# Order of the next stage's weight casts, a short chain moved to GpSimd, and a one-row product made square, in a two-layer hybrid decoder step

## The chip, the core and the metric

The kernel runs on one core of a Trainium2 chip. The metric is the device time of one execution in microseconds (us). Three runs of the kernel before gave 1076.46, 1076.46 and 1078.43 us, so the median is 1076.46 us.

## The reference, cut to what matters

A trunk of two layers is applied to 256 prompt tokens and 8 single sample tokens, so 264 columns in all, with 1024 features. Each layer is

```python
h = layer_norm(DN_ALPHA * x + 0.5 * swiglu(x, f1g, f1u, f1d), ln1_g, ln1_b)
mix = mixer(h, ...)                 # gated DeltaNet on 4 heads beside causal pooling
h = layer_norm(DN_ALPHA * h + mix, ln2_g, ln2_b)
y = layer_norm(DN_ALPHA * h + 0.5 * swiglu(h, f2g, f2u, f2d), ln3_g, ln3_b)

def swiglu(x, wg, wu, wd):
    return (jax.nn.silu(x @ wg) * (x @ wu)) @ wd
```

The hidden width of the SwiGLU is 2816. In the mixer every token and head has a decay

```python
g = -jnp.exp(a_log) * jax.nn.softplus(a_raw + dt_bias)
```

whose running sum inside a chunk sets the factors of the scores, and the mixer ends in `concatenate([o_dn, o_pool]) @ w_out`. All inputs are float32.

## The kernel before, in words

Features lie on the 128 partitions and tokens on the free axis, so an activation is eight tiles of 128 x 264. Every product is done in three parts in the type fp32r: each operand is split into a rounded high part and a low remainder (`mm3`, lines 220 to 223: high times high, high weight times low input, low weight times high input).

**Weights.** `Weights.load` brings a unit of 1 MB from memory into one of three `wraw` buffers by a transfer on the queue of SyncE, and splits its two pieces: the high part by a copy on ScalarE (`whi` or `xhi`, line 180), the low part by a subtraction on VectorE (`wlo` or `xlo`, line 185). `W.ahead(n)` loads until n pieces are ready and not yet taken by `W.get`. Pieces named `x..` are the first five of a stage and have buffers of their own; the others share three pairs. `W.after` and `W.after_hi` name an instruction of VectorE and of ScalarE behind which the subtractions and copies of the loads that follow are queued on that engine.

**Order of work.** TensorE runs its instructions in the order in which the source gives them. The other engines' orders are made by a planner from priorities (place in the source, raised inside `tc.high_priority()`) and from its own costs, and each engine then runs its queue in that fixed order.

**End of a feed-forward block** (`ffn`). Eight output tiles `pd` are made in turn, each of 22 x 3 matmuls with 22 pieces of the down weights in all. After each tile the residual sum is made in `X` (line 299, VectorE), and `Norm.shifted` makes from it `RH` (line 272, ScalarE), `RL` (line 273, VectorE), the square `sq` (lines 269 and 276, ScalarE), and the sums over tiles `acc1` (line 283) and `acc2` (line 285). `RH` and `RL` are the high and low parts of the sum before normalisation. The next stage starts on them at once: `raw_products` multiplies the first weight pieces by tiles that are already there, and `stats` (lines 345 and 346) then turns `acc1` and `acc2` into mean and variance by two products with ones. In a mixer the order is: 21 matmuls of the first piece `x0`, the statistics, then pieces `x1` to `x3`. In the feed-forward block of layer 1 it is: 24 matmuls that take turns between `x0` and `x1`, the statistics, then the rest.

At the tile m = 6 the kernel before calls `W.ahead(6)`. There 1 piece is ready, so three units are loaded: the last two of the down weights and the first of the next stage (`x0`, `x1`). After the last tile `W.ahead(4)` loads the second (`x2`, `x3`).

**The decay.** In the mixer, after the products of `q` tile 0 and pooling tile 3, the softplus is worked out on 128 x 12 numbers (lines 649 to 673): exponentials on ScalarE, and on VectorE a quotient `s_` (lines 662 to 664), a polynomial `p_` of its square `y_` (lines 665 to 669) and the sum `xa` (671) and product `gg` (673). From `gg` come `gp` (677, 678), the masked tiles `gm` (709) and four-head products `pdiff` (719) on TensorE. In the source these lie between four `q` and four pooling products; the convolutions `c` (line 528) and low parts `wlo` (185) run on VectorE meanwhile, and the window sums `wsum` (line 617) on GpSimd. `dm` (628 to 633) on VectorE reads `wsum`.

**The shift.** Eight output products `pop` (`w_pool`) of a layer start with `norm.less_shift`, a product that adds one row `less` (1 x 264) to all partitions: its stationary operand is one row of ones of `gto`. It has one row of contraction.

Of the kernel before, what the change touches and what calls it, by code (L numbers as in the profile page):

```python
# [10 lines left out]
F32R = mybir.dt.float32r  # L11
AF = mybir.ActivationFunctionType
ALU = mybir.AluOpType
# [3 lines left out]
P = 128  # L17
D = 1024
KD = D // P
SEQ = 256  # L20
NB = 8
T = SEQ + NB
# [3 lines left out]
H = 4  # L26
ALPHA = (2.0 * DEPTH) ** 0.25
# [63 lines left out]
def trunk(ctx: ExitStack, tc: tile.TileContext, a: dict):  # L91
    nc = tc.nc
    cpool = ctx.enter_context(tc.tile_pool(name="cpool", bufs=1))
    wpool = ctx.enter_context(tc.tile_pool(name="wpool", bufs=1))
    lpool = ctx.enter_context(tc.tile_pool(name="lpool", bufs=1))
# [10 lines left out]
    RH = cpool.tile([P, KD, T + 2], F32R, name="RH")  # L106
    RL = cpool.tile([P, KD, T + 2], F32R, name="RL")
    onr = cpool.tile([P, P], F32R, name="onr")
    gto = cpool.tile([P, 2, P], F32R, name="gto")
# [10 lines left out]
    def behind(ins):  # L120
        return nullcontext() if ins is None else tc.issue_after(ins.ins)

    def tables(name):
        tc.keep_in_program_order(nc.scalar.preload_act_table_set(name))
# [92 lines left out]
    W = Weights(units)  # L217
# [23 lines left out]
    class Norm:  # L241
# [22 lines left out]
        def shifted(self, m, eng1, eng2):  # L264
            y = X[:, m, :]
            sq = lpool.tile([P, T], F32, name="sq", tag="sq", bufs=4)
            late = self.fold and m > 5
            if not late and not self.behind_weights:
                nc.scalar.activation(sq, y, AF.Square)
            if self.fold:  # L270
                with tc.high_priority() if self.behind_weights else nullcontext():
                    nc.scalar.activation(RH[:, m, 0:T], y, AF.Copy, scale=self.g(m))
                    self.rl_op = nc.vector.scalar_tensor_tensor(RL[:, m, 0:T], y, self.g(m), RH[:, m, 0:T].bitcast(F32),
                                                                ALU.mult, ALU.subtract)
            if late or self.behind_weights:
                nc.scalar.activation(sq, y, AF.Square)
            if m == 0:
                self.sq0 = sq
            elif m == 1:
                eng1.tensor_add(self.acc1, X[:, 0, :], y)  # L280
                eng2.tensor_add(self.acc2, self.sq0, sq)
            elif m < KD - 1 or self.fold:
                eng1.tensor_add(self.acc1, self.acc1, y)
                with behind(self.rl_op if late else None):
                    (eng2 if m < KD - 1 else nc.vector).tensor_add(self.acc2, self.acc2, sq)
            else:
                self.last = sq
# [34 lines left out]
        def centre(self):  # L322
            p = psa.tile([P, T], F32, name="psh", tag="ax")
            for k in range(2):
                nc.tensor.matmul(p, onr, HH[:, k, :], start=k == 0, stop=k == 1)
            self.less = lpool.tile([P, T], F32R, name="less", tag="shift")[0:1]
            nc.scalar.activation(self.less, p[0:1], AF.Copy, scale=-4.0 * ALPHA)

        def less_shift(self, ps):

            nc.tensor.matmul(ps, gto[0:1, 0], self.less, start=True, stop=False)

        def add(self, m, ps):
            if m == 0:
# [94 lines left out]
    def ffn(src, norm, xnext, late=False):  # L429
        with tc.tile_pool(name="fp", bufs=1, reuse_waits="tile") as fp:  # L430
            gh = [fp.tile([P, T], F32R, name=f"gh{m}") for m in range(KF)]
            gl = [fp.tile([P, T], F32R, name=f"gl{m}") for m in range(KF)]

            def gate(m, y, bias, u, ubias):
                sg = fp.tile([P, T], F32, name="sg", tag="sg", bufs=2)
                gt = fp.tile([P, T], F32, name="gt", tag="gt", bufs=2)
                if bias is None:
                    with behind(hi1 if src is None and m == 0 else None):
                        nc.scalar.activation(sg, y, AF.Silu)
                    nc.vector.tensor_mul(gt, sg, u)  # L440
                else:
                    nc.scalar.activation(sg, y, AF.Silu, bias=bias)
                    nc.vector.scalar_tensor_tensor(gt, u, ubias, sg, ALU.add, ALU.mult)
                split(gh[m], gl[m], gt)

            first = 0
            if src is not None:
                W.ahead(6)
                raw = src.raw_products("gugugu", [((0,), 0, 6), ((1,), 0, 6), ((2,), 0, 6), ((3,), 0, 6), None,
                                                  ((0, 1, 2, 3), 6, KD), ((4, 5), 0, KD)] if late else  # L450
                                                 [((0, 1), 0, 4), None, ((0, 1), 4, KD), ((2, 3), 0, KD), ((4, 5), 0, KD)])
                src.normalise()
                W.after, W.after_hi = src.y_op, src.exp_op
                tables("silu_and_others")
                W.ahead(2)
                W.after = W.after_hi = None

                ws = [W.get(), W.get()]
                ps = [psa.tile([P, T], F32, name="p" + nm, tag="ax") for nm in "gu"]
                for k in range(KD):  # L460
                    for p, w in zip(ps, ws):
                        mm3(p, w, k, HH[:, k, :], HL[:, k, :], k == 0, k == KD - 1)
                W.ahead(2)
                for m in range(3):
                    gate(m, *src.settle(raw[2 * m]), *src.settle(raw[2 * m + 1]))
                gate(3, ps[0], None, ps[1], None)
                first = 4
            for m in range(first, KF):
                W.ahead(4)
                if src is None and m == 4:  # L470
                    constants_in()
                if src is None and m == 0:
                    pg, pu = two_products("gu")
                else:
                    pg = product(W.get(), "g")
                    pu = product(W.get(), "u")
                gate(m, pg, None, pu, None)
            tables("natural_log_exp_and_others")
            w, i = None, 0
            for m in range(KD):  # L480
                W.ahead(6 if m == 6 and xnext else 4)
                if m > 2:
                    norm.before(m, 2.0 * ALPHA)
                ps = psm.tile([P, T], F32, name="pd", tag="mm")
                for k in range(KF):
                    if i % KD == 0:
                        w = W.get()
                    mm3(ps, w, i % KD, gh[k], gl[k], k == 0, k == KF - 1)
                    i += 1
                    if m == 2 and k == 10:  # L490
                        norm.shift2()
                        norm.before(m, 2.0 * ALPHA)
                norm.add_scaled(m, ps, 2.0 * ALPHA)
                if m == KD - 1 and xnext:
                    W.ahead(4)


    def mixer(l, src, norm, xstack):
        with tc.tile_pool(name="mp", bufs=1, reuse_waits="tile") as mp:
# [147 lines left out]
            with tc.high_priority():  # L647
# [3 lines left out]
                nega = mp.tile([P, H], F32, name="nega")  # L651
# [3 lines left out]
                xa, e_, s_, y_, p_ = sc("xa"), sc("e_"), sc("s_"), sc("y_"), sc("p_")  # L655
# [5 lines left out]
                nc.scalar.activation(beta, bat[:, :, 0:4], AF.Exp, scale=-1.0)  # L661
                nc.vector.tensor_scalar_add(s_, e_, 2.0)
                nc.vector.reciprocal(s_, s_)
                nc.vector.tensor_mul(s_, s_, e_)
                nc.vector.tensor_mul(y_, s_, s_)
                nc.vector.tensor_scalar_mul(p_, y_, 1.0 / 15.0)
                for n in (13, 11, 9, 7, 5, 3):
                    nc.vector.scalar_tensor_tensor(p_, p_, 1.0 / n, y_, ALU.add, ALU.mult)
                nc.vector.scalar_tensor_tensor(p_, p_, 1.0, s_, ALU.add, ALU.mult)
                nc.vector.tensor_scalar_max(xa, xa, 0.0)  # L670
                nc.vector.scalar_tensor_tensor(xa, p_, 2.0, xa, ALU.mult, ALU.add)
                gg = sc("gg")
                nc.vector.tensor_mul(gg, xa, nega.unsqueeze(1).to_broadcast([P, 3, H]))
                nc.vector.tensor_scalar_add(beta, beta, 1.0)
                nc.vector.reciprocal(beta, beta)
                gp, gms = mp.tile([P, 2, 2, H], F32, name="gp"), {}
# [453 lines left out]
            for x in range(2):  # L1130
                for j in range(2):
                    p = psa.tile([64, 2, 64], F32, name="pU", tag="ax")
                    sl = slice(64 * j, 64 * j + 64)
                    for i in range(2):
                        nc.tensor.matmul(p[:, i, :], Q[x][sl, 2 * i + j, :], two(W2[x], i)[sl, 64:P],
                                         start=True, stop=True)
# [12 lines left out]
            p = psa.tile([P, H, P], F32, name="pu1", tag="ax")  # L1149
# [6 lines left out]
            p = psa.tile([P, H, P], F32, name="pmu", tag="ax")  # L1156
# [37 lines left out]
            p = psa.tile([P, HB], F32, name="pod", tag="ax")  # L1194
# [6 lines left out]
            p = psa.tile([P, H, P], F32, name="pu2", tag="ax")  # L1201
# [20 lines left out]
            p = psa.tile([P, H, P], F32, name="psf", tag="ax")  # L1222
# [37 lines left out]
            for m in range(KD):  # L1260
# [6 lines left out]
                if m % 2 == 0:  # L1267
                    ps = [psm.tile([P, T], F32, name="pout", tag="mm") for _ in range(2)]
# [138 lines left out]
```

## Time and profile before

| | |
|---|---|
| median of three runs | 1076.46 us |
| profiled execution, its own time | 1076.49 us |
| span of its instructions | 1074.7 us |
| TensorE busy | 1049.0 us, 98% of the span |
| VectorE busy | 752.9 us, 70% |
| ScalarE busy | 596.8 us, 56% |
| GpSimd busy | 155.3 us, 14% |
| mean granted TensorE clock | 0.995 |

The span runs from the first to the last instruction; 1.8 us of the execution lie around it. A busy TensorE isn't one at its peak, since matmuls overlap: the distance between two starts tells the rate, and the duration of one is longer than that. Granted clock 1.00 is 2.4 GHz. In the views, L185 is line 185 of the kernel, `out<-in` are the program's tile names, and a bracket at the end of a row tells how long the engine was idle before it and which instruction ended that.

### The profile page before, as it was taken

To read this page: it belongs to the slowest core of one execution; us is meant where nothing else is said; L and a number is where in the kernel's file an instruction comes from. 1 tells how busy PE (TensorE), PEld (TensorE's weight loads), DVE (VectorE), ACT (ScalarE), POOL (GpSimd) and SP (SyncE) were. 2 spreads that over 40 slices of the span, in tenths; PEclk is the share of its full clock that TensorE was granted. 3 is DMA by queue.
4 is the path that set the end of the run, shared out by engine and by line. 5 is a ranking of instruction groups with operands and counts; after the bars stand their busy time and mean duration, and the time that the engine had idled before them with its cause. 6 is when DMAs were issued, how large, how long until landed. Compare 5 with 4: busy or idle time off the path is not lost.

```text
span 1074.7 us, 20803 instructions
## 1 busy us (share of the span) xinstructions
PE 1049.0 (98%) x8434; PEld 1031.1 (96%) x8434; DVE 752.9 (70%) x1223; ACT 596.8 (56%) x1081; POOL 155.3 (14%) x206
## 2 busy tenths in 40 slices
PE   9999999999999999999999999999899999999995
PEld 8999999999889999999999999999898999999995
DVE  5555557989779955557785555778997898555554
ACT  6444444668936744444574444466587476444442
POOL 0000012233340000003200000321433200000131
PEclk9999999999999999999999999999999999999998
DMA  8554545833234454544625454466331345455441
GB/s 306 193 182 174 194 158 197 299 102 114 98 138 167 148 190 174 196 169 184 246 93 205 167 194 181 173 235 222 134 121 62 135 168 189 167 194 179 174 157 41
DMA packets 35839, 183.23 MB, mean 170 GB/s; under 512 B 6816, under 2 KB 12576, under 8 KB 15520
## 3 DMA queue, kind: packets, MB, share of 16 engines
q1 hardware_dynamic: 28672, 175.19, 44.3%
q10 hardware_dynamic: 7072, 6.72, 1.8%
q8 instruction: 66, 1.08, 0.4%
q14 instruction: 29, 0.24, 0.1%
HBM read 175.18 MB, written 6.72 MB: 169 GB/s over the span
## 4 chain that ended last, share of the span: by engine, by line
PE 87%; DVE 7%; DMA 2%; issue 2%; ACT 1%; POOL 1%; ACTq 0%; SPq 0%; DVEq 0%; POOLq 0%
PE pd L221 8%; PE pd L223 7%; PE pd L222 7%; PE pu L223 7%; PE pu L222 7%; PE pu L221 7%; PE pg L222 7%; PE pg L221 7%; PE pg L223 7%; DVE wlo L185 1%; DVE xlo L185 1%; PE pop L221 1%; PE pP L1041 1%; POOL wsum L617 1%; PE pout L222 1%
## 5 line engine op out<-in xcount | busy, mean ns | idle before, releaser
L185 DVE TENSOR_TENSOR wlo<-wraw,whi 128x1024 fp32r<-128x1024 f32 (+1 forms) x301 | 368.0, 1226 | 202.8 <-ACT whi L180 202.4
L180 ACT ACTIVATE whi<-wraw 128x1024 fp32r<-128x1024 f32 (+1 forms) x301 | 312.4, 1041 | 326.3 <-issue 117.0
L221 PE MATMUL pd<-gh,whi 128*128 128x264 f32 x704 | 200.3, 285 | 0.0
L223 PE MATMUL pd<-gh,wlo 128*128 128x264 f32 x704 | 199.9, 284 | 0.0
L222 PE MATMUL pd<-gl,whi 128*128 128x264 f32 x704 | 198.8, 282 | 0.0
L221 PE MATMUL pg<-HH,whi 128*128 128x264 f32 x632 | 179.6, 284 | 0.7 <-ACT whi L180 0.7
L222 PE MATMUL pg<-HL,whi 128*128 128x264 f32 x632 | 179.5, 284 | 0.7 <-DVE HL L381 0.7
L223 PE MATMUL pu<-HH,wlo 128*128 128x264 f32 x632 | 179.2, 284 | 0.8 <-DVE wlo L185 0.8
L223 PE MATMUL pg<-HH,wlo 128*128 128x264 f32 x632 | 179.4, 284 | 0.5 <-DVE wlo L185 0.5
L221 PE MATMUL pu<-HH,whi 128*128 128x264 f32 x632 | 179.3, 284 | 0.0
L222 PE MATMUL pu<-HL,whi 128*128 128x264 f32 x632 | 179.1, 283 | 0.0
L222 PEld LDWEIGHTS pd<-gl,whi 128*128 128x128 f32 x704 | 132.5, 188 | 0.0
L223 PEld LDWEIGHTS pd<-gh,wlo 128*128 128x128 f32 x704 | 132.5, 188 | 0.0
L221 PEld LDWEIGHTS pd<-gh,whi 128*128 128x128 f32 x704 | 132.4, 188 | 0.0
L222 PEld LDWEIGHTS pg<-HL,whi 128*128 128x128 f32 x632 | 119.2, 189 | 1.2 <-DVE HL L381 1.2
L221 PEld LDWEIGHTS pg<-HH,whi 128*128 128x128 f32 x632 | 119.1, 189 | 1.0 <-ACT whi L180 1.0
L223 PEld LDWEIGHTS pu<-HH,wlo 128*128 128x128 f32 x632 | 118.5, 187 | 1.2 <-DVE wlo L185 1.2
L223 PEld LDWEIGHTS pg<-HH,wlo 128*128 128x128 f32 x632 | 118.6, 188 | 1.0 <-DVE wlo L185 0.8
L222 PEld LDWEIGHTS pu<-HL,whi 128*128 128x128 f32 x632 | 119.1, 188 | 0.0
L221 PEld LDWEIGHTS pu<-HH,whi 128*128 128x128 f32 x632 | 119.0, 188 | 0.0
L305 POOL TENSOR_TENSOR s<-X 128x264 fp32r<-128x264 f32 x4 | 3.0, 759 | 632.2 <-DVE X L302 632.2
L440 DVE TENSOR_TENSOR gt<-sg,pu 128x264 f32<-128x264 f32 x79 | 33.8, 428 | 50.8 <-PE pu L223 50.8
(374 smaller groups left out, 2003.7 us busy)
## 6 DMA issues: line engine op xcount, KB each, us to landing
wraw<-in_f_gu SPq DMA_DIRECT2D x86, 1024.0 KB, 4.8
wraw<-in_f_d SPq DMA_DIRECT2D x44, 1024.0 KB, 4.8
wraw<-in_w_in SPq DMA_DIRECT2D x20, 1024.0 KB, 4.9
wraw<-in_w_out SPq DMA_DIRECT2D x8, 1024.0 KB, 4.9
S<-in_sdelta SPq DMA_DIRECT2D x8, 512.0 KB, 6.7
out_o_ds<-S ACTq DMA_DIRECT2D x8, 512.0 KB, 2.6
X<-in_xT ACTq DMA_DIRECT2D x4, 264.0 KB, 5.6
out_o_y<-X SPq DMA_DIRECT2D x4, 264.0 KB, 2.4
```

Source lines behind the costliest of these rows:

```text
L180: self.last_hi = nc.scalar.activation(h, r, AF.Copy)
L185: nc.vector.tensor_sub(l, r, h.bitcast(F32))
L221: nc.tensor.matmul(ps, hi[:, k, :], xh, start=first, stop=False)
L222: nc.tensor.matmul(ps, hi[:, k, :], xl, start=False, stop=False)
L223: nc.tensor.matmul(ps, lo[:, k, :], xh, start=False, stop=last)
L305: nc.gpsimd.tensor_add(self.s2, X[:, 0, :], X[:, 1, :])
L440: nc.vector.tensor_mul(gt, sg, u)
L617: nc.gpsimd.tensor_add(nx[:, lo + d:], cur[:, lo + d:], cur[:, lo:EXT - d])
L1041: nc.tensor.matmul(two(p, i), two(N[x][lv], i), halves(Tm[x][:, 2 * i:2 * i + 2, :], 1 << lv, 0), start=True, stop=True)
```

## The change

It has three parts.

1. In `ffn`, where another stage follows, the load at m = 6 falls from `W.ahead(6)` to `W.ahead(4)` and the call at m = 7 is left out. After the last tile `W.ahead(4)` stays, but with `W.after` set to the instruction that makes `RL` of that tile and `W.after_hi` to the one that makes `RH`. With one piece ready at m = 6 and five taken in m = 6 and 7, none is ready after the last tile, so this call now loads two units, `x0` to `x3`, and all their copies and subtractions stand behind `RH` and `RL` of the last tile on their engines. This holds at three places: before each mixer, and before the feed-forward block that opens layer 1.
2. The softplus from `s_ = s_ * e_` to `gg` goes from VectorE to GpSimd. The fused steps (add, then multiply) become two instructions, so that 12 instructions of VectorE become 20 of GpSimd in each layer.
3. `less` keeps all 128 partitions, scaled by 8 times as much, and is multiplied by `onr`, the 128 x 128 matrix of 1/1024. The sum over 128 equal rows gives the same value as before.

```diff
                 with tc.high_priority() if self.behind_weights else nullcontext():
-                    nc.scalar.activation(RH[:, m, 0:T], y, AF.Copy, scale=self.g(m))
+                    self.rh_op = nc.scalar.activation(RH[:, m, 0:T], y, AF.Copy, scale=self.g(m))
...
-            self.less = lpool.tile([P, T], F32R, name="less", tag="shift")[0:1]
-            nc.scalar.activation(self.less, p[0:1], AF.Copy, scale=-4.0 * ALPHA)
+            self.less = lpool.tile([P, T], F32R, name="less", tag="shift")
+            nc.scalar.activation(self.less, p, AF.Copy, scale=-32.0 * ALPHA)
...
-            nc.tensor.matmul(ps, gto[0:1, 0], self.less, start=True, stop=False)
+            nc.tensor.matmul(ps, onr, self.less, start=True, stop=False)
...
-                W.ahead(6 if m == 6 and xnext else 4)
+                if m < KD - 1 or not xnext:
+                    W.ahead(4)
...
                 if m == KD - 1 and xnext:
+                    W.after, W.after_hi = norm.rl_op, norm.rh_op
                     W.ahead(4)
+                    W.after = W.after_hi = None
...
-                nc.vector.tensor_mul(s_, s_, e_)
-                nc.vector.tensor_mul(y_, s_, s_)
-                nc.vector.tensor_scalar_mul(p_, y_, 1.0 / 15.0)
+                nc.gpsimd.tensor_mul(s_, s_, e_)
+                nc.gpsimd.tensor_mul(y_, s_, s_)
+                nc.gpsimd.tensor_scalar_mul(p_, y_, 1.0 / 15.0)
                 for n in (13, 11, 9, 7, 5, 3):
-                    nc.vector.scalar_tensor_tensor(p_, p_, 1.0 / n, y_, ALU.add, ALU.mult)
-                nc.vector.scalar_tensor_tensor(p_, p_, 1.0, s_, ALU.add, ALU.mult)
+                    nc.gpsimd.tensor_scalar_add(p_, p_, 1.0 / n)
+                    nc.gpsimd.tensor_mul(p_, p_, y_)
+                nc.gpsimd.tensor_scalar_add(p_, p_, 1.0)
+                nc.gpsimd.tensor_mul(p_, p_, s_)
                 nc.vector.tensor_scalar_max(xa, xa, 0.0)
-                nc.vector.scalar_tensor_tensor(xa, p_, 2.0, xa, ALU.mult, ALU.add)
+                nc.gpsimd.tensor_scalar_mul(p_, p_, 2.0)
+                nc.gpsimd.tensor_add(xa, p_, xa)
                 gg = sc("gg")
-                nc.vector.tensor_mul(gg, xa, nega.unsqueeze(1).to_broadcast([P, 3, H]))
+                nc.gpsimd.tensor_mul(gg, xa, nega.unsqueeze(1).to_broadcast([P, 3, H]))
```

## Rows read from the trace of the kernel before

**Rows 1.** The page, part 1: busy time, share of the span, instructions.

```profile
PE 1049.0 (98%) x8434; PEld 1031.1 (96%) x8434; DVE 752.9 (70%) x1223; ACT 596.8 (56%) x1081; POOL 155.3 (14%) x206
```

**Rows 2.** Waits of TensorE: waited for; us in total, times, longest.

```profile
PE pq L223 <- DVE wlo L185: 4.2, 2, 2.1
PE ps L346 <- DVE acc L285: 3.1, 2, 1.7
...
PE pdiff L719 <- DVE gm L709: 1.3, 1, 1.3
```

**Rows 3.** Timeline of TensorE, both mixers' starts: start, us, instruction, [idle before].

```profile
199.93 0.28 PE L221 MATMUL pk<-RH,xhi 128*128 128x266 f32 x1
...
204.86 0.71 PE L346 MATMUL ps<-acc,cst 128*128 128x264 f32 x2 [1.73 <-DVE acc L285]
205.22 0.48 PE L221 MATMUL pk<-RH,xhi 128*128 128x266 f32 x1
...
731.98 0.71 PE L346 MATMUL ps<-acc,cst 128*128 128x264 f32 x2 [1.42 <-DVE acc L285]
```

**Rows 4.** Timeline of VectorE, end of layer 0's first feed-forward block.

```profile
200.13 0.43 DVE L299 TENSOR_TENSOR X<-pd,X 128x264 f32<-128x264 f32 x1 [0.41 <-PE pd L223]
...
201.42 2.35 DVE L185 TENSOR_TENSOR wlo<-wraw,whi 128x1024 fp32r<-128x1024 f32 x2
203.69 0.60 DVE L273 SCALAR_TENSOR_TENSOR RL<-X,sm,RH 128x264 fp32r<-128x264 f32 x1
204.21 0.60 DVE L285 TENSOR_TENSOR acc<-acc,sq 128x264 f32<-128x264 f32 x1
```

**Rows 5.** Timeline of ScalarE, end of layer 0's second feed-forward block.

```profile
531.66 1.06 ACT L180 ACTIVATE xhi<-wraw 128x1024 fp32r<-128x1024 f32 x1 [2.01 <-DMA wraw<-in_f_gu]
...
535.49 0.52 ACT L272 ACTIVATE RH<-X,sm 128x264 fp32r<-128x264 f32 x1 [1.82 <-DVE X L299]
535.91 0.41 ACT L276 ACTIVATE sq<-X 128x264 f32<-128x264 f32 x1
```

**Rows 6.** Timeline of TensorE around one shift product, layer 0.

```profile
291.48 0.38 PE L761 MATMUL psc<-c,c 128*128 128x256 f32 x1
291.69 0.38 PE L762 MATMUL psc<-c,c 128*128 128x128 f32 x2
292.01 0.38 PE L331 MATMUL pop<-less,gto 1*128 1x264 f32 x1
292.32 0.39 PE L221 MATMUL pop<-RH,whi 128*128 128x264 f32 x1
292.54 0.28 PE L222 MATMUL pop<-RL,whi 128*128 128x264 f32 x1
292.67 0.28 PE L223 MATMUL pop<-RH,wlo 128*128 128x264 f32 x1
```

**Rows 7.** Busy time by stretch, both layers; after POOL's: granted clock, DMA share, GB/s.

```profile
238.00:242.00 4.00, 4.00 (x23) 4.00 (x22) 4.00 (x11) 1.49 (x5) 1.50 (x2) 0.57 0.44 127
...
766.00:770.00 4.00, 4.00 (x34) 3.90 (x33) 4.00 (x11) 2.21 (x8) 2.30 (x1) 1.00 0.69 219
```

**Rows 8.** Timeline of VectorE in layer 0's decay.

```profile
226.36 0.21 DVE L663 RECIPROCAL s__2714<-s__2714 128x12 f32<-128x12 f32 x1
...
239.66 0.15 DVE L673 TENSOR_TENSOR gg<-xa,nega 128x12 f32<-128x12 f32 x1
```

**Rows 9.** Instructions on one tile: ns minimum/median/maximum, first and last start.

```profile
L668 DVE SCALAR_TENSOR_TENSOR p__2716<-p__2716,y__2715 x6: 153/156/800, 232.7 to 237.4; 128x12 f32<-128x12 f32 x6
```

**Rows 10.** Timeline of TensorE at the first decay products, layer 0.

```profile
244.26 0.69 PE L719 MATMUL pdiff<-gm,gto 128*128 128x512 f32 x2
```

**Rows 11.** Timeline of GpSimd: window sums, and dependent small products later.

```profile
226.10 3.11 POOL L617 TENSOR_TENSOR wsum<-wsum 128x396 f32<-128x396 f32 x3
...
298.81 0.25 POOL L936 TENSOR_TENSOR us<-us,ab 128x32 f32<-128x32 f32 x1
299.14 0.25 POOL L938 TENSOR_TENSOR qk<-qk,us 128x32 f32<-128x32 f32 x1
```

## The prediction, written before the changed kernel was run

> **What bounds the kernel now.** I read the page first: TensorE is busy for 98% of the span [rows 1]. A view that adds durations can't say more of an engine so full, so next come the waits of TensorE alone. There are three that matter, each at the same place in both layers: `pq` in the mixer waits for a `wlo` of VectorE, 2.1 us each time; the second statistics product waits for `acc`, 1.7 and 1.4 us; and `pdiff` waits 1.3 us for `gm`, in one layer only [rows 2, 3]. All else of TensorE's time is matmuls back to back. So an edit counts if it takes matmul time away, ends one of these waits, or makes a new one. The three parts of the change touch these places one by one, and the stages between them shift as a whole.
>
> **Part 1, the weight pieces after the last tile.** In the kernel before, TensorE goes from the last `pd` to the first `pk` without a pause, at 199.93, because `x0` was split long before [rows 3]. Then it runs 21 matmuls, and waits for `acc`, whose queue on VectorE holds two `wlo` in front of `RL` and `acc` [rows 4]. With the change those can't stand there, and `acc` is ready about 2 us sooner. But `x0` is then split only behind `RH` and `RL` of the last tile, and TensorE needs `x0` first. I count from the start of the first matmul of the next stage (0). `X` starts at +0.20 and takes 0.43 [rows 4]. In the hand-over of layer 0's second block ScalarE is free for the last tile: `RH` takes 0.52, `sq` starts 0.42 behind it and takes 0.41 [rows 5]. So `RH` runs from +0.66, `sq` from +1.08, and the copy `xhi0` of 1.06 [rows 5] from +1.40 to +2.46; I let `sq` go first, since it has the raised priority. Low parts take 1.18 each (2.35 for two, [rows 4]): `xlo0` ends at +3.65, `xlo1` at +4.8.
>
> At a mixer two matmuls go at +2.46, and the third waits for `xlo0`. The other 19 at 0.12 each (the distance of the matmuls in [rows 6]) end at +5.95. Four statistics steps, of which the last two take 0.36 [rows 3], make 0.7, and the second `pk` starts at +6.65. Before, it was 205.22 - 199.93 = +5.29. So layer 0 loses 1.4 us although its old wait is gone, and layer 1, whose old wait was 0.3 us shorter, 1.7 [rows 3]. At the feed-forward block of layer 1, where no wait stood [rows 2], the matmuls of `x0` and `x1` take turns: the sixth needs `xlo1`, at +4.8 in place of +0.6. That loses 4.2. The sum is 1.4 + 1.7 + 4.2 = 7.3 us. If `xhi0` goes before `sq` it is about 1 us less.
>
> Then the clock. Behind the wait of 2.1 us in layer 0 the granted clock has a mean of 0.57 over 4.00 us [rows 7]: it falls to the lower level, 1.2 GHz, and 4.00 x 0.43 = 1.7 us are lost. The equal wait in layer 1 leaves it at 1.00 [rows 7]. The new waits are 2.5 us, two matmuls, and 1.2 us more; the third is longer still. The cost lies between none and three times 1.7. I take two of the three, 3.4 us. Part 1 then costs 10.7 us, between 6.3 and 12.4.
>
> The pieces that follow (the third and fourth units) get their buffers later too, and are split while the layer norm fills ScalarE and VectorE, where before they ran in the wait. TensorE needs them only some twenty us later, so I take nothing; if that cover fails, it is up to the 2.35 us of one pair [rows 4] in each mixer. No transfer is added; on SyncE's queue those of the fourth unit on wait for a buffer longer, and what stands behind them there (the mixer's states) with them.
>
> **Part 2, the softplus on GpSimd.** What waits is `gg`. It ends at 239.81 in layer 0 [rows 8], and `pdiff` starts 4.45 us behind it, at 244.26 [rows 10]; in layer 1 TensorE waits there already [rows 2]. So this stretch is set by `gg`, not by the `pq` wait ahead of it, and it moves only as far as `gg` moves. GpSimd can begin when the reciprocal ends, at 226.57 [rows 8]. Dependent small products there start 0.33 apart [rows 11] (of 32 numbers a partition; here 12, so this is a bound from above if nothing disturbs). Twenty are 6.6 us. Alone they would end at 233.2. But GpSimd also has the window sums: three of one pooling tile take 3.1 us [rows 11], and those of the next tile come before 239 too, at the same price. With both between, `gg` is ready at 226.57 + 6.6 + 3.1 + 3.1 = 239.4. That is where it was. VectorE loses 12 small instructions, of 0.16 us mostly [rows 9], which helps its `wlo`; that helps TensorE reach `pdiff` earlier and wait there.
>
> I take 0. The lower bound is `gg` so early that the `pq` and `pdiff` waits all go: 2.1 + 1.7 of clock in layer 0, 2.1 + 1.3 in layer 1, so -7.2 [rows 2, 7]. The upper bound comes from what the two engines do to each other. One and the same `L668` takes between 153 and 800 ns [rows 9], the long ones while a window sum runs. At 0.65 for each of twenty it would be 13 us a layer; at a quarter of that, since VectorE's operations are mostly shorter than a window sum, it is 3 us a layer, +6 in all.
>
> **Part 3, the shift.** A matmul of 264 columns starts 0.12 to 0.13 behind its forerunner (292.54 to 292.67). The one-row product holds the next for 0.31 us, and the next holds its follower for 0.22, so 0.29 are lost; and the two 128-column steps in front of it take 0.32, where one of 256 columns takes 0.21, so 0.11 more [rows 6]. With 128 rows the product is like its neighbours, and 0.39 us go, 16 times: 6.2 us. Nothing waits in that stretch [rows 2], so all are on TensorE's path; but it holds the triangular inverse, a chain through VectorE and ScalarE between which these products are filling, and a shorter filling can end in a wait. Bounds are half (3.1) and all (6.2); I take three quarters, 4.7. ScalarE's `less` on 128 partitions takes no longer than on one, as other copies of 264 columns show (0.41 for `sq`, [rows 5]).
>
> **The sum.** 1076.49 for the profiled execution (span 1074.7 and 1.8 around it; the median of the runs is 1076.46, the same) + 10.7 + 0 - 4.7 = 1082.5 us.
>
> **The rivals.**
>
> *GpSimd's chain runs ahead of the window sums.* Then `gg` comes before 236 and the waits in the middle of the mixers go: 1076.49 + 7.3 - 4.7 - 7.2 = 1071.9, if the clock stays up behind the new waits. It decides from 2.4 us a layer on (`gg` before 237.4); if the clock falls it does not suffice. For it: priority is raised for the softplus and not for the sums. Against it: each step depends on the last, and on VectorE the planner put other work between such steps.
>
> *VectorE and GpSimd hold each other up.* `gg` comes 3 us later in each layer: 1082.5 + 6 = 1088.5. For it: 153 against 800 ns [rows 9]. Against it: only some of the small operations were held.
>
> The Trainium skill ("SBUF — State Buffer", Who interferes with whom) says that a VectorE instruction with two inputs in SBUF contends with a GpSimd instruction that reads SBUF, and that the later one is blocked until the first ends. By that rule this rival would be likelier than I make it; the 800 ns agree, the 153 ns come from times without a window sum.
>
> *Part 1 costs its least and part 3 gives its most.* No clock falls, all 16 products count: 1076.49 + 7.3 - 6.2 = 1077.6, no difference.
>
> **How the numbers follow.** The forecast has 0.56, the early chain 0.14, the mutual hold-up 0.15, the wash 0.15. About 0.2% (2.2 us) is what a measurement of this kernel can tell from no change. Faster by more is the early chain, 0.14; within it is the wash, 0.15; slower by more is the rest, 0.71. The forecast's own range is 1079 to 1086. The range of 8 in 10 takes in the wash, half of the early chain, and the hold-up: 1073 to 1090.
>
> **What would show it.** The waits of TensorE should have new rows at three places: the first `pk` for `xhi` (about 2.4 us) and `xlo` (about 1.2) in both mixers, and the first `pg` and `pu` in layer 1; the wait for `acc` should be gone. If TensorE goes into the next stage without a pause, part 1 is wrong. The shift product should have neighbours 0.12 apart; if its 0.31 stays, one row was not the reason. `gg` should end about 13.2 us behind the reciprocal, as before [rows 8]; if it comes over 2.4 us sooner and `pq` no longer waits, the early chain holds. Granted clock below 1.00 in stretches right behind the new waits would show the 3.4 us.

## The result, and the profile after

The changed kernel takes **1108.14 us** (median of 4 runs, 1106.1 to 1108.59) where the kernel before takes 1076.46 us beside it: a ratio of 1.029, 95% interval 1.0277 to 1.0303. That is 31.7 us slower. The forecast was 1082.5 us with a range up to 1090: the sign was right, the size was not. The profiled execution took 1108.08 us, with a span of 1106.3.

Page of the kernel after, part 1 (engine, busy time, share of the span, instructions); it answers to [rows 1]:

```profile
PE 1056.0 (95%) x8434; PEld 1039.2 (94%) x8434; DVE 747.6 (68%) x1199; ACT 595.5 (54%) x1081; POOL 174.4 (16%) x246
```

TensorE issues as many instructions as before. It is busy 7 us longer, at a mean granted clock of 0.978 in place of 0.995, and the span is 31.6 us longer: most of the loss is waits. These are the waits of TensorE, after (answer to [rows 2]: waited for; us in total, times, longest):

```profile
PE pq L223 <- DVE wlo L185: 10.5, 2, 5.2
PE pq L221 <- ACT ext L614: 6.7, 2, 3.3
PE pk L221 <- ACT xhi L180: 6.2, 2, 3.2
PE pk L223 <- DVE xlo L185: 3.2, 2, 1.6
...
PE pg L221 <- ACT xhi L180: 3.0, 1, 3.0
```

`pk` and `pg` are part 1's places, and they were forecast. The two rows of `pq`, 17.2 us together where the kernel before has 4.2 [rows 2], are part 2's, and nothing of the kind was forecast. The wait for `acc` is gone, as expected, and so is that of `pdiff`.

To see where the time is lost, I compare the start of the same matmul in the two traces. The step in the shift is what a stretch cost.

| matmul | before | after | later by | the stretch cost |
|---|---|---|---|---|
| a `pq` behind the layer norm, layer 0 | 216.14 | 223.09 | 6.95 | part 1, mixer 0: 6.8 (0.1 stood before) |
| first `pdiff`, layer 0 | 244.26 | 258.50 | 14.24 | part 2: 7.3 |
| first `pg` of the second block, layer 0 | 339.89 | 352.12 | 12.23 | part 3: -2.0 |
| a `pg` ahead of the statistics, layer 1's first block | 536.45 | 555.43 | 18.98 | part 1, feed-forward: 6.75 |
| a `pq` behind the layer norm, layer 1 | 743.26 | 769.20 | 25.94 | part 1, mixer 1: 7.0 |
| first `pv`, layer 1 | 773.69 | 806.92 | 33.23 | part 2: 7.3 |
| first `pg` of the second block, layer 1 | 867.09 | 898.62 | 31.53 | part 3: -1.7 |

Part 1 cost 20.5 us (forecast 10.7), part 2 14.6 (forecast 0), part 3 gave 3.7 (forecast 4.7).

**Part 1 in rows.** TensorE at the start of mixer 0, after (answer to [rows 3]):

```profile
199.91 0.28 PE L223 MATMUL pd<-gh,wlo 128*128 128x264 f32 x1
203.38 0.39 PE L221 MATMUL pk<-RH,xhi 128*128 128x266 f32 x1 [3.19 <-ACT xhi L180]
203.61 0.29 PE L222 MATMUL pk<-RL,xhi 128*128 128x266 f32 x1
205.51 0.59 PE L223 MATMUL pk<-RH,xlo 128*128 128x266 f32 x1 [1.61 <-DVE xlo L185]
205.90 0.43 PE L221 MATMUL pk<-RH,xhi 128*128 128x266 f32 x1
206.12 0.43 PE L222 MATMUL pk<-RL,xhi 128*128 128x266 f32 x1
```

Two matmuls, then a second wait, then matmuls 0.22 us apart in place of 0.12. The two waits have the expected order, and each is 0.9 us longer than worked out. Counted by starts, as the prediction counts, the first matmul could have started 0.12 us behind the last `pd`, at 200.03. It starts 3.35 us later, where 2.46 was worked out, and the third starts 2.13 us behind the first, where 1.19 was. ScalarE, then VectorE in the same stretch show why (the latter answers to [rows 4]):

```profile
202.29 3.88 ACT L180 ACTIVATE xhi<-wraw 128x1024 fp32r<-128x1024 f32 x4
```

```profile
199.95 1.23 DVE L185 TENSOR_TENSOR xlo<-wraw,xhi 128x1024 fp32r<-128x1024 f32 x1 [5.25 <-ACT xhi L180]
201.10 0.43 DVE L299 TENSOR_TENSOR X<-pd,X 128x264 f32<-128x264 f32 x1
...
201.51 1.22 DVE L185 TENSOR_TENSOR wlo<-wraw,whi 128x1024 fp32r<-128x1024 f32 x1
202.64 0.98 DVE L273 SCALAR_TENSOR_TENSOR RL<-X,sm,RH 128x264 fp32r<-128x264 f32 x1
...
204.07 5.36 DVE L185 TENSOR_TENSOR xlo<-wraw,xhi 128x1024 fp32r<-128x1024 f32 x4
```

Counted from 200.03, `X` starts at +1.07, not +0.20: a low part of the third unit (`x4`), which the change leaves without a dependency, stands in front of it, and its neighbour in front of `RL`. The four copies of `x0` to `x3` run without a pause behind `sq`, so their transfers had landed: their place in the queue made them late, not the later load. The clock, by stretch, after (answer to [rows 7]; the last three numbers are the granted clock, the DMA share and GB/s):

```profile
204.00:208.00 4.00, 2.49 (x11) 2.49 (x12) 4.00 (x4) 2.31 (x4) 3.77 (x4) 0.50 0.79 274
...
550.00:554.00 4.00, 3.01 (x12) 2.39 (x12) 4.00 (x5) 2.38 (x3) 0.00 (x0) 0.50 0.70 262
...
750.00:754.00 4.00, 2.39 (x12) 2.39 (x12) 4.00 (x4) 2.42 (x4) 3.77 (x4) 0.50 0.83 270
...
250.00:255.00 5.00, 3.92 (x18) 3.92 (x19) 5.00 (x9) 0.00 (x0) 3.78 (x2) 0.50 0.37 111
```

Behind the waits at each of the three places, and behind part 2's, TensorE runs at the lower of its levels, 1.2 GHz (0.50).

**Part 2 in rows.** ScalarE, then VectorE, then TensorE in layer 0, after:

```profile
243.42 0.21 ACT L683 ACTIVATE gp<-gg 128x8 fp32r<-128x8 f32 x1 [8.97 <-POOL gg L679]
...
243.63 1.04 ACT L180 ACTIVATE whi<-wraw 128x1024 fp32r<-128x1024 f32 x1
244.57 0.36 ACT L612 ACTIVATE ext<-pp 128x256 f32<-128x256 f32 x1
```

```profile
243.66 1.29 DVE L715 TENSOR_TENSOR gm<-cst,gp 128x512 fp32r<-128x512 f32 x2 [4.99 <-ACT gp L683]
...
249.81 2.35 DVE L185 TENSOR_TENSOR wlo<-wraw,whi 128x1024 fp32r<-128x1024 f32 x2
```

```profile
245.04 0.59 PE L221 MATMUL pq<-HH,whi 128*128 128x264 f32 x1 [3.33 <-ACT ext L614]
...
251.08 0.59 PE L223 MATMUL pq<-HH,wlo 128*128 128x264 f32 x1 [5.23 <-DVE wlo L185]
```

ScalarE stands for 8.97 us with `gp` at the head of its queue. It waits for `gg`, and behind it are the copy `whi` and the evacuation `ext` that TensorE needs. VectorE stands for 4.99 us at `gm`, with two low parts behind it that TensorE needs next; they read `whi`, so they hang on ScalarE's stand too. In the kernel before, `gp` stood too, but three copies `whi` and two evacuations (`ext` and a `c`) further back in the queue, and VectorE did not stand. That row, from before:

```profile
239.84 0.21 ACT L677 ACTIVATE gp<-gg 128x8 fp32r<-128x8 f32 x1 [4.18 <-DVE gg L673]
```

GpSimd, which does the work now, isn't slow:

```profile
237.64 1.10 POOL L672 TENSOR_TENSOR p__2716<-p__2716,y__2715 128x12 f32<-128x12 f32 x1
...
243.18 0.21 POOL L679 TENSOR_TENSOR gg<-xa,nega 128x12 f32<-128x12 f32 x1
245.07 0.85 POOL L620 TENSOR_TENSOR wsum<-ext 128x398 f32<-128x398 f32 x1 [1.69 <-ACT ext L614]
```

`gg` ends at 243.39, 10.6 us behind the end of the reciprocal (232.76); before it was 13.2 [rows 8]. The window sums of the next pooling tile start only behind it: their `ext` stood behind `gp` on ScalarE.

### The profile page after: what moved, and what is told of

Read it like the earlier page. It is cut to its first block, busy times and chain, and to the rows that moved or that the text cites. A ratio compares the mean times of both kernels' runs of the same rounds, so it can differ in the third digit from the quotient of the medians.

```text
span 1106.3 us, 20819 instructions
## 1 busy us (share of the span) xinstructions
PE 1056.0 (95%) x8434; PEld 1039.2 (94%) x8434; DVE 747.6 (68%) x1199; ACT 595.5 (54%) x1081; POOL 174.4 (16%) x246
## 4 chain that ended last, share of the span: by engine, by line
PE 80%; DVE 10%; DMA 3%; ACT 3%; issue 2%; POOL 1%; ACTq 0%; DVEq 0%; POOLq 0%
PE pu L223 7%; PE pu L222 7%; PE pu L221 7%; PE pg L222 7%; PE pg L221 7%; PE pg L223 7%; PE pd L221 7%; PE pd L223 7%; PE pd L222 7%; DVE wlo L185 2%; DMA wraw<-in_w_in 2%; POOL wsum L620 1%; DVE xlo L185 1%; DMA wraw<-in_f_gu 1%; DVE X L366 1%
```

## The experiments

The theory after the comparison: (a) the parts add up; (b) part 1 loses because `x0` and `x1` are split too late, not because `x2` and `x3` are queued behind `RL` and `RH`; (c) part 2 loses because the readers of `gg` stand too early in two in-order queues; (d) part 3 works because of the 128 rows. Rival to (c): GpSimd and VectorE hold each other up. The kernel before took 1076.07 to 1076.13 us on the same chips.

### Each part alone

e1 has only the edits of part 1, e2 only those of part 2, e3 only those of part 3.

> Part 1 alone (order of the weight casts). My reading of the changed kernel's trace: each of the three hand-overs moves by 6.7 to 7 us, so +20 us against the kernel before (1096 to 1098). Rival: only the waits for x0 and x1 count (the 7.3 us of the prediction) and the rest of the shift at the hand-overs comes from parts 2 and 3: then +7 to +9 us.

> Part 2 alone (softplus on GpSimd). From the changed kernel's trace: each mixer moves by 7.3 us between q tile 0 and the decay products, so +14 to +15 us. Rival: the waits there are an after-effect of part 1's later casts (the third and fourth weight units come late); then part 2 alone costs under 3 us.

> Part 3 alone (square shift product). From the changed kernel's trace: 14.2 falls to 11.7 us of shift over the eight products of a layer, then 0.5 comes back, so -2 us a layer, -4 in all. Rival: all of 16 x 0.39 = 6.2 us is gained where nothing else disturbs: -6.

| run | us | ratio, 95% interval | against before |
|---|---|---|---|
| e1, part 1 | 1096.81 | 1.0194, 1.0179 to 1.0209 | +20.7 |
| e2, part 2 | 1091.17 | 1.0138, 1.0123 to 1.0153 | +15.0 |
| e3, part 3 | 1072.22 | 0.9963, 0.9949 to 0.9977 | -3.9 |

The sum is +31.8, and the whole change +31.7. The parts add up, so each can be studied alone.

### Part 1: what is late, and what it costs

e7 keeps the loads at m = 6 and m = 7 as they were, so that `x0` and `x1` are split early, and the dependency holds only for `x2` and `x3`:

```diff
-                if m < KD - 1 or not xnext:
-                    W.ahead(4)
+                W.ahead(6 if m == 6 and xnext else 4)
```

> Part 1 with the loads at m = 6 and 7 left as before (x0, x1 split in time), and only x2, x3 behind RH and RL of the last tile. Theory: the loss of part 1 is that x0 and x1 are not ready; so nothing is left of it: -2 to +1 us against the kernel before. The wait for acc stays, since the two low parts in front of RL belong to a later unit. Rival: the dependency itself costs, by what it pushes into the layer norm: +3 us or more.

It took 1078.55 us (ratio 1.0023, 1.0013 to 1.0032): 18.3 of the 20.7 us are gone, so (b) holds. The dependency of `x2` and `x3` alone costs about 2.4, between the expected -2 to +1 and the rival's 3 or more. e7 loads `x0` and `x1` earlier and takes them out of the dependency in one; the two are not parted by a run, but by the copies above, which did not wait for their transfers.

e8 asks for the clock's share: part 1, and 24 matmuls whose result nobody reads fill the wait.

```diff
                     W.after = W.after_hi = None
+                    pb = psa.tile([P, T], F32, name="pbusy", tag="ax")
+                    for n in range(24):
+                        nc.tensor.matmul(pb, RL[:, 0, 0:P], RL[:, 1, 0:T], start=True, stop=True)
```

> Part 1 with 24 matmuls more between the last pd and the first product of the next stage, whose result nobody reads (2.9 us in what is a wait of 3.0 to 3.2 us). Theory: about 2.4 to 3.3 us at each of the three places are the clock at its lower level behind the wait; with TensorE busy the 21 to 24 matmuls behind it start 0.12 apart and the time falls from 1096.8 to 1087 to 1091. Rival: those matmuls are slow because their operands come late; then the time stays within 2 us of part 1.

It took 1095.47 us (1.0169, 1.0154 to 1.0184), only 1.3 better than e1: the value that the rival gave, though not for the rival's reason. Stretches of e8, columns as above:

```profile
204.00:208.00 4.00, 2.46 (x20) 2.46 (x21) 4.00 (x4) 2.34 (x4) 3.76 (x4) 1.00 0.81 263
...
544.00:548.00 4.00, 3.50 (x17) 3.29 (x18) 3.23 (x3) 0.96 (x2) 0.00 (x0) 0.65 0.84 317
...
748.00:752.00 4.00, 4.00 (x24) 3.80 (x23) 2.90 (x6) 1.64 (x4) 0.56 (x1) 0.75 0.94 340
```

In mixer 0 the clock stayed at 1.00, and the matmuls behind the second wait started 0.12 us apart. From the first `pk` to the statistics e1 lost 3.6 us against before, and e8 2.0, so the clock cost 1.6 there. At the other two places it fell even so. In the feed-forward block TensorE stood for 1.2 and 0.5 us for `xlo`, behind its first two and its fifth matmul. In mixer 1 it stood for 1.4 us between the filling and the first matmul, which came 1.3 us later than in e1, and for 1.6 behind the second. So the clock's price is shown at one place of three; the waits themselves are not mended by filling. In the feed-forward block the sixth matmul comes 5.4 us late in e8 as in the changed kernel, though e8's granted clock is 1.00 up to there: this lateness is the wait for `x0` and `x1`, not the clock.

e11 takes up the low parts in front of `X` and `RL`: part 1, with the third unit behind `RL` and `RH` too.

```diff
+            W.after, W.after_hi = src.rl_op, src.rh_op
             W.ahead(2)
+            W.after = W.after_hi = None
             src.normalise()
```

> Part 1 alone (1096.8 us), with the third unit of each mixer (x4 and its neighbour) queued behind RL and RH of the last tile too. In part 1 its low part of 1.2 us stood in front of X of the last tile and another in front of RL. If these casts are what made the new waits 3.2 and 1.6 us where 2.5 and 1.2 were worked out, the time falls by 2 to 4 us, to 1093 to 1095. Rival, that x0's copy waits for other work on ScalarE: 1096 to 1098.

It took 1095.69 us (1.0181, 1.0167 to 1.0195): 1.1 better than e1, less than expected, with intervals that overlap. Its waits tell why:

```profile
PE pq L223 <- DVE wlo L185: 6.3, 2, 3.2
PE pk L221 <- ACT xhi L180: 4.7, 2, 2.3
...
PE pk L223 <- DVE xlo L185: 1.5, 2, 0.7
```

The first two waits of a mixer are now 2.3 and 0.7 us, in e1 3.0 and 1.5 (mean). By starts, the first matmul comes at +2.49 and the third 1.26 us behind it, in both mixers: nearly the 2.46 and 1.19 that the prediction had worked out. What was won there is paid later: `pq` waits 3.2 us for a `wlo` where e1's wait was 1.7. The third unit's low parts have to run somewhere, and they now run late.

e10 keeps the idea for pieces that TensorE needs late. It is the kernel before with part 3, and with only the load of the first q tile (the two `wlo` in front of `RL` and `acc`, [rows 4]) queued behind `RL` and `RH`:

```diff
+            W.after, W.after_hi = src.rl_op, src.rh_op
             q_tile(0, pq)
+            W.after = W.after_hi = None
```

> Kernel before with the square shift product, and, in place of part 1, only the load of the first q tile of each mixer (the two pieces that stood ahead of RL and acc of the last tile) queued behind RL and RH of the last tile. x0 to x3 are loaded early, as before. Theory that part 1's idea was sound for pieces that TensorE needs late, and wrong for x0 and x1: the waits for acc (1.7 and 1.4 us) go, nothing new comes, 1072.2 - 3.1 = 1069.1 us, 1068 to 1071. Rival, that the two pieces then come too late for the q products behind the layer norm: 1072 to 1076.

It took **1070.64 us** (0.9948, 0.9934 to 0.9961), within the expected range, and is faster than both kernels. Against e3 it is 1.6 us, half of the 3.1 that stood in the wait for `acc`. That wait is gone (the `pk` behind the statistics starts 1.7 us sooner than in e3 in mixer 0, and 1.9 in mixer 1), and 1.2 us of it come back in each mixer in the first products behind the layer norm, at `pba` and `pq`. Of its waits:

```profile
PE pq L223 <- DVE wlo L185: 3.5, 2, 1.8
...
PE pba L559 <- DVE HL L381: 0.9, 2, 0.4
```

### Part 2: the queue or the engines

e4 takes part 2 alone and queues the readers of `gg` later: `gp` and `as_` behind the evacuation of pooling tile 1 on ScalarE, `gp`, `gm` and `ad` behind the last low part loaded in q tile 2 on VectorE. e5 puts `dm` of pooling tile 2 there as well (the second piece of the cut below). e6 is e5 with the softplus left on VectorE.

```diff
+            with tc.issue_after(ext_op[1].ins), tc.issue_after(lo5.ins):
+                gp, gms = ...            # moved here from the place behind gg
...
+            with tc.issue_after(lo5.ins):
+                map2 = p_map(2)
```

> Part 2, but the instructions that read gg (gp, as_ on ScalarE; gp's low part, ad, gm on VectorE) are queued behind the copies, evacuations and low parts of the q and pooling tiles. Theory: the loss of part 2 is these readers standing at the head of two in-order queues while GpSimd works, so nearly all of it goes: -2 to +2 us against the kernel before, and no wait of TensorE over 1 us between q tile 0 and the decay products. Rival: GpSimd's chain itself, or VectorE and GpSimd holding each other up, is what costs; then the time stays within 3 us of part 2 alone.

> As the last run (softplus on GpSimd, readers of gg queued late), and the dm instructions of pooling tile 2 too, behind the same low part. Theory: what was left there is VectorE standing 5.6 us at dm, whose window sums wait behind the softplus on GpSimd. Then the wait of pp for wlo (5.2 and 5.5 us) goes, and since gg itself ends about 2 us sooner than before, the time comes to 1071 to 1077, at or below the kernel before. Rival: what is left is contention of the two engines; then it stays at 1084 to 1088.

> The same queue order (readers of gg and dm late) with the softplus left on VectorE: the control for the last run. If the order of the two queues is all that counts, it is as fast as that run within 2 us; if GpSimd's shorter chain (gg 2 us sooner) is worth something once the queues are mended, it is 2 to 5 us slower than that run. Against the kernel before -2 to +2 us.

All three came out otherwise than expected: e4 took 1086.35 us (1.0094, 1.0079 to 1.0109), e5 1092.78 (1.0152, 1.0137 to 1.0167), e6 1086.7 (1.0094, 1.0077 to 1.0111). In e4 VectorE no longer stands at `gm`, and ScalarE stands for 1.6 us at `gp` in layer 0 in place of 8.8 (e2); the next instruction in line took their place. VectorE, e4:

```profile
239.71 0.41 DVE L628 SCALAR_TENSOR_TENSOR dm<-wsum,ext 128x240 f32<-128x240 f32 x1 [5.58 <-POOL wsum L617]
```

The window sums of pooling tile 2 now wait on GpSimd behind the whole softplus, so their reader `dm` holds VectorE. In e5 `dm` and a low part stand in front of `gm`, and in e6, where no GpSimd chain is left, the second pair of `gm` is late too, behind two low parts. First wait of TensorE in e5, and in e6:

```profile
PE pdiff L726 <- DVE gm L716: 18.0, 4, 6.4
```

```profile
PE pdiff L723 <- DVE gm L713: 10.3, 2, 5.1
```

So the right place for `gm` is narrow: too early and it holds what TensorE needs, too late and `pdiff` waits. e6 costs 10.6 us with no work moved at all.

e9 puts the readers where they stood in the kernel before: `gp` behind the evacuation of pooling tile 1, `gm` behind the third low part after the reciprocal, `dm` of pooling tile 2 behind `gm`. e13 is the same with the softplus on VectorE.

```diff
             p_tile(1)
+            with tc.issue_after(ext_op[1].ins), tc.issue_after(W.los[-2].ins):
+                gp, gms = ...            # moved here, and the loop of gm behind it
             q_tile(3)
-            map2 = p_map(2)
+            with tc.issue_after(gm_op.ins):
+                map2 = p_map(2)
```

> Softplus on GpSimd (part 2 alone, 1091.2 us), with its readers queued at the place that they had in the kernel before: ScalarE's gp behind the evacuation of pooling tile 1, VectorE's gp and gm behind the third low part after the reciprocal and the taps of q tile 2, and dm of pooling tile 2 behind gm, so that nothing that TensorE needs stands behind a reader of gg or of the late window sums. Theory that part 2 costs its 15 us by the place of the readers in the two in-order queues: gg is ready near 236.5 in layer 0, the waits of pq and pp for ext and wlo fall under 2.5 us each, and the time is 1069 to 1077. Rival, that GpSimd and VectorE hold each other up: gg or gm is late wherever the readers stand, and the time stays above 1084, as in the two tries before.

> The softplus stays on VectorE; the queue edits are those of the run with the readers at their old place (1082.7 us with the softplus on GpSimd). Theory that the 6.6 us left there are GpSimd's own: its chain takes 10.4 us there, where VectorE is busy, against 7.1 us where VectorE stood still, and gm and gp take longer beside the window sums behind the chain: 1074 to 1078 here, since nothing of that is left. Rival, that they are the new queue places (a low part between the gm, dm behind them): 1081 to 1084 here too.

e9 took 1082.67 us (1.0060, 1.0046 to 1.0074), between what the two theories gave: 8.5 of part 2's 15 us are gone with the places alone. e13 took 1080.98 us (1.0044, 1.0033 to 1.0054), the rival's value: of e9's 6.6 us, 4.9 come from the places, which are not quite those of before (a low part stands between the two pairs of `gm`, and `pdiff` waits 2.0 us for the second). **With the same places, the softplus costs 1.7 us more on GpSimd than on VectorE**, by medians whose intervals overlap a little. In layer 0 `gg` ends at nearly the same time, at 239.20 on VectorE (e13) and 239.06 on GpSimd (e9). VectorE in e9, and in e13:

```profile
239.34 2.34 DVE L707 TENSOR_TENSOR gm<-cst,gp 128x512 fp32r<-128x512 f32 x2 [0.87 <-ACT gp L693]
241.60 0.80 DVE L694 TENSOR_TENSOR gp<-gg,gp 128x8 f32<-128x8 f32 x1
```

```profile
241.30 1.27 DVE L704 TENSOR_TENSOR gm<-cst,gp 128x512 fp32r<-128x512 f32 x2
242.50 0.15 DVE L691 TENSOR_TENSOR gp<-gg,gp 128x8 f32<-128x8 f32 x1
```

In e9 the late window sums run on GpSimd beside these, and the same instructions take 3.14 us in place of 1.42. But they start 2.0 us sooner, since VectorE has less in front of them, so the second pair of `gm` is not later for it (243.55 in e9, 243.81 in e13). The 1.7 us stand elsewhere. TensorE at its second `pdiff` and in the stretch behind it, in e9 and in e13:

```profile
244.28 0.79 PE L725 MATMUL pdiff<-gm,gto 128*128 128x512 f32 x1 [3.30 <-DVE gm L707]
244.00:248.00 4.00, 3.72 (x9) 2.96 (x10) 4.00 (x9) 1.30 (x3) 3.92 (x2) 0.50 0.17 27
```

```profile
244.54 0.50 PE L722 MATMUL pdiff<-gm,gto 128*128 128x512 f32 x1 [2.02 <-DVE gm L704]
244.00:248.00 4.00, 3.46 (x20) 3.10 (x21) 4.00 (x9) 1.05 (x3) 1.84 (x2) 1.00 0.08 15
```

In e9 TensorE no longer waits for a `wlo` in `pq` (3.3 us in e13, both layers). So it is at `pdiff` sooner and waits there longer, and behind that wait the granted clock is 0.50; in e13 it stays at 1.00. Layer 1 is alike (waits of 1.2 and 3.3 us, then 0.65 over 776 to 780). TensorE's waits in `pq`, `pdiff`, `pz` and `py` together are no longer in e9 (8.9 us) than in e13 (9.2). What e9 costs over e13 is thus, for the most part, the slower matmuls behind one longer wait.

e14 asks whether e13's places help the best version (e10 with e13's edits).

> The square shift product, the q tile's two pieces behind RL and RH (1070.6 us together), and the queue edits of the run above with the softplus on VectorE. If those edits end the pq waits (1.8 us and the clock behind the first) and cost nothing at gm: 1066 to 1070. If what they win at pq they lose at pdiff: 1070 to 1073. If they cost by themselves: above 1075.

It took 1076.99 us (1.0005, 0.9995 to 1.0014), above e10 by 6.4: by themselves these places cost, as in e13. TensorE waits 4.0 us in all for the second `gm`, and 2.8 us in `pUt` for `V` of ScalarE, a wait that e10 does not have.

### Part 3: is it the number of rows?

e12 is part 3 with 64 rows, which are equal, in place of 128.

```diff
-            nc.tensor.matmul(ps, onr, self.less, start=True, stop=False)
+            nc.tensor.matmul(ps, onr[0:64], self.less[0:64], start=True, stop=False)
```

> Part 3 alone with 64 equal rows in place of 128 (scale doubled). If any number of rows under 128 holds up the neighbours as one row did, the gain of 3.9 us is gone: 1075 to 1077. If only a small operand did it, the gain stays: 1072 to 1073. In the trace, the neighbours of the shift product then are 0.31 or 0.12 us away.

It took 1076.48 us (1.0007, 0.9998 to 1.0016): nothing is left of the gain. TensorE around the shift product, e3 and then e12 (answers to [rows 6]):

```profile
291.67 0.37 PE L331 MATMUL pop<-less,onr 128*128 128x264 f32 x1
291.87 0.29 PE L221 MATMUL pop<-RH,whi 128*128 128x264 f32 x1
292.00 0.28 PE L222 MATMUL pop<-RL,whi 128*128 128x264 f32 x1
```

```profile
292.11 0.39 PE L331 MATMUL pop<-less,onr 64*128 64x264 f32 x1
292.43 0.39 PE L221 MATMUL pop<-RH,whi 128*128 128x264 f32 x1
292.65 0.28 PE L222 MATMUL pop<-RL,whi 128*128 128x264 f32 x1
```

With 64 rows the distances are 0.32 and 0.22, as with one row [rows 6]; with 128 they are 0.20 and 0.13. So it isn't that there is one row. That it isn't the low number of rows either, a place in the kernel before shows, where three products of 8 rows follow each other:

```profile
221.46 0.35 PE L571 MATMUL pbt<-cst,bar 8*128 8x8 f32 x3
221.74 0.39 PE L221 MATMUL pp<-HH,whi 128*128 128x264 f32 x1
```

They start 0.08 and 0.06 us apart. Held up are the first of them (0.21 behind a product of 128 rows, in place of 0.12) and the second product of 128 rows behind them (0.22). What costs is that the shape differs from its neighbours'. The Trainium skill ("TensorEngine Tiling (Array Packing)", Key Properties; Available Configurations) says that changing the tiling mode drains TensorE, and lists 64 rows as another configuration than 128; these rows agree.

## Why the prediction was wrong

- **Reading the kernel by TensorE's waits: right.** All that was lost lies at the starts of the stages and between the `q` products, where the prediction looked.
- **Part 1, the mechanism: right; the sizes: half.** The step "`X` starts at +0.20" failed. It carried over the row of before, but the third unit's low parts now stand in front of `X` and `RL`, and `X` starts at +1.07 in mixer 0, at +0.87 in mixer 1 and at +0.86 in the feed-forward block; without them, in e11, the two waits of a mixer are as worked out. By the comparison of starts, the waits for `x0` and `x1` cost 3.5 and 3.6 us in the mixers up to the third matmul, with the old `acc` waits taken off (forecast 1.4 and 1.7), and 5.4 in the feed-forward block up to the sixth (forecast 4.2): 12.5 in place of 7.3. The slower matmuls behind them cost 2.1, 2.1 and 1.4, so 5.6 (forecast 3.4: two places of three at 1.7; it was all three). The step "I take nothing" for the third and fourth units failed too: 1.2 us are lost behind the layer norm in each mixer, 2.4 in all. These make the 20.5. The upper bound of 12.4 was too low because it left the waits and this last term at their single values.
- **Part 2, the failed step: "this stretch is set by `gg` ... and it moves only as far as `gg` moves".** It priced the chain and left the queues as they were. `gg` did come sooner, 10.6 us behind the reciprocal in place of 13.2. That is more than the 2.4 us from which the rival of the early chain was to win, and yet the kernel lost. The planner's order changed with the edit: it put `gp` and `gm` further forward in the queues of ScalarE and VectorE, and each engine stood with TensorE's next operands behind. TensorE then waited at `pq`, ahead of `pdiff`, 7.1 us more in each layer than before. The prediction named what stands behind a late instruction for VectorE's `acc` and didn't ask it of `gp` and `gm`, though ScalarE's stand at `gp` can be read in the trace of before.
- **Part 2 at other places: near the forecast, in part by luck.** With the readers of `gg` where e9 and e13 have them, the move costs 1.7 us where 0 was taken, and in layer 0 `gg` is "where it was" to 0.14 us. The sum behind that was another: 3.6 us of window sums stood in front of the chain in e9, which then took 10.4; worked out were 6.6 for the chain and two sets of sums at 3.1. (The sums of that pooling tile are four instructions, not three; the first takes 1.4 us more.) That a lighter VectorE "helps TensorE reach `pdiff` earlier and wait there" came true in e9, and the clock behind that longer wait is most of the price, which the prediction did not ask for.
- **The clock in the lower bound of part 2 was no loss.** It counted 1.7 us for the slow stretch behind `pq` in layer 0. In e3 the granted clock stays at 1.00 there, and TensorE then waits 1.34 us for `gm`: its second `pdiff` starts at 244.17, and in the kernel before at 244.50 without a wait. A slow stretch in front of a wait costs little.
- **The rival of mutual hold-up** is real in the rows; its share of the kernel's time is not shown. The Trainium skill ("SBUF — State Buffer", Who interferes with whom) says that the later of the two engines is blocked; the trace agrees: a small product of GpSimd takes 0.21 us, and 1.10 beside a low part. The chain from `s_` to the end of `gg` takes 7.1 us in e2, where VectorE stands still for 4.7 of them, and 10.4 in e9, where it works (`s_` starts at 229.23 and 228.65, `gg` ends at 236.34 and 239.06). In e9 it also takes back 1.7 of the 2.0 us by which `gm` starts sooner. Between e5 and e6 the softplus on GpSimd costs 6.1 us, with `dm` waiting for the late sums in it. The two aren't parted further.
- **Part 3: right, somewhat less.** Each product gave 0.37 us (3.0 over the eight of layer 0), as worked out (0.39). In each layer 0.4 us came back at `pku` and 0.6 at `pout`, where short waits now stand (0.3 and 0.1 us): the "shorter filling that can end in a wait". 3.9 us were measured (e3), 4.7 taken, within 3.1 to 6.2. ScalarE's `less` does take longer on 128 partitions than on one, 0.45 us against 0.36, but TensorE never waits for it.

## What to carry to other kernels

Before a step is moved to another engine, list its readers and what stands behind them in their in-order queues: the move may change that order, and a sooner result at the head of a standing queue can cost more than a later one further back (in layer 0 `gg` ended at 236.3 in e2, which lost 15.0 us, and at 239.1 in e9, which lost 6.6). Queue behind the critical chain only pieces that are needed late (e10), and never the first operand of the next stage. Keep the shape of a filler product like its neighbours'.

## What the runs showed of the hardware

- A product of 64 rows between products of 128 holds its neighbours up as much as one of a single row (0.32 and 0.22 us between starts, against 0.20 and 0.13).
- A GpSimd product of 12 numbers a partition takes 0.21 us alone and 1.10 beside VectorE work on two inputs; in the other direction, a VectorE instruction of 8 numbers takes 0.15 us alone and 0.80 beside a window sum.
- Products of 8 rows that follow each other aren't held up (0.08 and 0.06 us between starts); the change of shape is.
- Two waits of 3.2 and 1.6 us, with two matmuls between, leave TensorE at 1.2 GHz behind them (0.50 of the full clock over 4 us). A wait of 1.6 us alone, with matmuls up to its beginning, left it at 1.00 (e8, mixer 0); waits of 1.4 and 1.6 us with two matmuls between did not (0.75 over 4 us, e8, mixer 1). Waits of 1.7 and, 8 us later, 2.0 us left it at 1.00 (e13), and waits of 0.5 and 3.3 us did not (0.50 over 4 us, e9).
